# One decoder layer on one core: the Strassen units of the input projection in two passes, one for each token half

## The chip, the core and the metric

The program runs on one core of a Trainium2 chip. The metric is the device time of one execution in microseconds (us), less is better. The engines are TensorE (PE in the profile; its weight loads are listed apart as PEld), VectorE (DVE), ScalarE (ACT), GpSimd (POOL) and SyncE (SP), which issues nearly all DMAs of this kernel. Each engine works through its own instructions in order; the DMAs that SP issues are carried out by 16 DMA engines while SP goes on.

## What is computed

One hybrid layer on 2048 tokens of width 1024, in float32. The part that the change touches is the normalisation, the big input projection and the attention branch that works beside it:

```python
h = rms_norm(x, norm_w[layer])
proj = h @ w_in[layer]                    # 1024 x 9224
(dn_qkv, dn_z, dn_b, dn_a, swa_q, swa_k, swa_v, swa_z, gates) = jnp.split(proj, split_points, axis=-1)
...
sq = partial_rope(rms_norm(grp(swa_q), q_norm_w[layer][:, None, :]), cos, sin)
sk = partial_rope(rms_norm(grp(swa_k), k_norm_w[layer][:, None, :]), cos, sin)
sv = grp(swa_v)
for gi, (window, dilation) in enumerate(SWA_GROUPS):   # (128, 1), (512, 4), (2048, 16)
    o_g, lse_g = dilated_window_attention(sq[:, :, gi], sk[:, :, gi], sv[:, :, gi], window, dilation)
...
merged = jax.nn.sigmoid(g_dn) * y_dn + jax.nn.sigmoid(g_swa) * y_swa
x = x + merged @ w_out[layer]
```

## The kernel before

**Products in three matmuls.** A float32 operand is split into a high part (a copy into a rounded format, made by ACT) and a low part (the difference, made by DVE or POOL). A product is then three matmuls: high by high, high by low, low by high. All products of the projection are made so.

**Stage 1, the first unit** (`first_unit`, L412 to L500): 16 tiles of 128 tokens, in the order `ORDER`, which takes tiles of the two quarters of a token half alternately. For each tile x is loaded twice, once by rows (`xt`, a single buffer, for the sum of squares, `x_nat` L117 and `x_stat` L129) and once by channels (`xc`, `x_chan` L122). The row factor goes through a diagonal matrix (`x_diag` L136) and a matmul with ones (`x_rows` L140) to DVE, which scales `xc` (`x_scale` L146). The scaled tile is split (`x_high` L164, `x_low`), multiplied with the columns of the values of attention group 2 (24 matmuls with 256 or 264 columns a tile), and combined with its partner tile into the sums S1 to S4 (`x_sums`, `x_put`). A token half has eight such operands, A11 to A22 and S1 to S4, in high and low parts of 1 MB each. Those of the first half (p = 0) stay in SBUF in `hh` and `hl` (place by `SLOT`), A21 apart, which goes to DRAM like everything of the second half (p = 1), L172, L206 and L207; seven of the first half are written to DRAM as well (`save` L98).

**Stage 2, sixteen units** (`seq`, `unit`): a unit makes 512 columns for one token half with Strassen's scheme in Winograd's form, seven products (`PROD`) of 48 matmuls with 256 columns (L391), so 336 a unit. The token half p alternates: two units of p = 0, five of p = 1, six of p = 0, three of p = 1. In the last unit before each change of p every product, once done, loads the other half's operand into its place from DRAM (`restore` L102); after the last unit the half that is missing comes back for stage 3. The weights of the products are computed two products ahead (`w_ahead`): four loads a unit (`w_load` L253), four sums and differences on DVE (`w_sums` L259), seven high parts on ACT (`w_high` L275) and seven low parts (`w_low` L282), three on DVE and four on POOL, into a ring of four places. Each column block is thus loaded and split twice, once for each token half. Query and key units normalise their result: squares on ACT (L326), a power on POOL (L327, L329), a scaling on DVE (L334), the rotation on POOL in two halves of four instructions each (`turn`, L346 to L349), then a store (L350).

**Attention beside it.** `hook` counts a tick after every six matmuls and then runs what is due. `att_loop` gives each attention item its four pieces (load and transposes, scores, transposes of p, product with v) in steps of three phases; a step takes four ticks, delays (1, 2, 1). `att_ready` lists the items of a head once its columns are there: group 2 after p = 1, group 1 after p = 0 (which comes after p = 1 there), group 0 for each half.

**Stage 3** (`cunits`, L659 to L661): 36 units of 128 columns by 2048 tokens, each with 96 matmuls of 512 columns, for the DeltaNet branch and the gates; its weights are loaded and split by `w128` into an own pool, which opens when the pools of stage 2 are closed. Beside it run the rest of the attention, the small vectors of the DeltaNet (`ab_math`, L693 on), its chunk inverses and its scan; then the output stage (L1170 to L1189).

PE, ACT, DVE and POOL run in the order in which the program is written in stages 1 and 2 (`pinned`); the order on SP is made by a scheduler.

## Time and profile before

| what | value |
|---|---|
| time, median of 3 runs | 2518.11 us (2513.8 to 2520.08) |
| the profiled execution, its time | 2515.84 us |
| its span, first to last instruction | 2513.9 us, granted PE clock 0.965 |
| stage 1: first matmul with x at 10.5 us, last at about 191 us | 16 tiles |
| stage 2: L391 from 191.8 us to about 1081 us | 16 units |
| stage 3: first L659 at 1109.7 us | 36 units |
| DMA traffic | 413.15 MB, 164 GB/s over the span |

Busy times count an instruction from its start to its end. The matmuls of PE overlap, so a PE that is always busy can still be given work faster or slower; the number of matmuls in a stretch of known length shows the pace better. An entry such as "idle before, releaser" names what ended the wait of an engine. The wait tables list, for a waiting engine and line, who released it, the total time, how often, and the longest.

### The profile page before, as it was taken

How to read it: one execution, taken by the hardware profiler on the slowest of the kernel's cores; microseconds unless marked ns; L12 is line 12 of the kernel's file. 1: busy time of each engine (PE TensorE's matmuls, PEld its weight loads, DVE VectorE, ACT ScalarE, POOL GpSimd, SP SyncE). 2: the span in 40 equal slices, each digit the busy share in tenths (PEclk: the TensorE clock that was granted, in tenths of full speed). 3: DMA queues.
4: the chain of work that ended last, by engine and by line, in shares of the span. 5: the costliest groups of instructions: out<-in, count | busy, mean ns of one | idle time of the engine just before them, and what ended most of it. 6: DMA issues, size and time to landing. Idle time of an engine off the chain costs nothing.

```text
span 2513.9 us, 43806 instructions
## 1 busy us (share of the span) xinstructions
PE 2330.1 (93%) x15184; PEld 2106.3 (84%) x15184; DVE 1389.9 (55%) x2882; ACT 959.6 (38%) x2976; POOL 1066.5 (42%) x1754
## 2 busy tenths in 40 slices
PE   7649799989999989969899999999999999999999
PEld 7649799979999889958677888888888878898998
DVE  6435466655565555652487777699824451444431
ACT  5324344543455554633566665111233322211110
POOL 5426884552852552630085566111223321443342
PEclk8879899999999999979999999999999999999999
DMA  8993835486344674563345444322377663655442
GB/s 256 303 346 113 320 119 153 134 314 180 104 143 135 218 255 136 164 196 105 107 128 132 127 118 109 110 72 76 112 197 213 187 195 117 185 153 179 148 134 80
DMA packets 460116, 413.15 MB, mean 164 GB/s; under 512 B 63544, under 2 KB 416120, under 8 KB 451064
## 3 DMA queue, kind: packets, MB, share of 16 engines
q1 hardware_dynamic: 459608, 410.29, 53.6%
q8 instruction: 121, 1.98, 0.3%
q14 instruction: 99, 0.81, 0.1%
q10 hardware_dynamic: 288, 0.07, 0.0%
HBM read 260.01 MB, written 150.24 MB: 163 GB/s over the span
## 4 chain that ended last, share of the span: by engine, by line
PE 58%; DMA 6%; POOL 5%; DVE 3%; ACT 3%; issue 2%; SPq 0%; POOLq 0%; ACTq 0%; DVEq 0%
PE mm L391 10%; PE mm L659 8%; PE mm L661 8%; PE mm L660 8%; PE mm L1189 2%; PE mm L1187 2%; PE mm L1188 2%; PE mm L1170 2%; PE mm L1172 2%; PE mm L1171 2%; DMA gcb<-gcscr 2%; DMA qk<-qks 2%; PE tp L523 1%; PE po L565 1%; POOL kql L863 1%
## 5 line engine op out<-in xcount | busy, mean ns | idle before, releaser
L659 PE MATMUL mm<-hh,wh 128*128 128x512 f32 x1152 | 466.9, 405 | 0.0
L661 PE MATMUL mm<-hh,wl 128*128 128x512 f32 x1152 | 456.5, 396 | 0.0
L660 PE MATMUL mm<-hl,wh 128*128 128x512 f32 x1152 | 452.7, 393 | 0.0
L391 PE MATMUL mm<-wh,hh 128*128 128x256 f32 x896 | 274.2, 306 | 9.3 <-ACT wh L275 9.3
L391 PE MATMUL mm<-wl,hh 128*128 128x256 f32 x896 | 259.4, 290 | 16.1 <-POOL wl L282 15.2
L391 PE MATMUL mm<-hh 128*128 128x256 f32 x896 | 270.1, 301 | 1.9 <-ACT hh L275 1.9
L84 POOL TENSOR_TENSOR wl<-raw,wh 128x512 fp32r<-128x512 f32 x72 | 104.0, 1457 | 388.1 <-ACT wh L83 387.8
L391 PE MATMUL mm<-hl,hh 128*128 128x256 f32 x896 | 254.6, 284 | 6.4 <-POOL hl L282 6.4
L391 PE MATMUL mm<-wh,hl 128*128 128x256 f32 x896 | 259.3, 289 | 0.0
L661 PEld LDWEIGHTS mm<-hh,wl 128*128 128x128 f32 x1152 | 217.8, 189 | 47.8 <-POOL wl L84 0.4
L391 PE MATMUL mm<-hh,hl 128*128 128x256 f32 x896 | 254.5, 284 | 0.0
L659 PEld LDWEIGHTS mm<-hh,wh 128*128 128x128 f32 x1152 | 218.6, 190 | 41.5 <-ACT wh L83 0.4
L660 PEld LDWEIGHTS mm<-hl,wh 128*128 128x128 f32 x1152 | 218.3, 190 | 41.6
L391 PEld LDWEIGHTS mm<-wl,hh 128*128 128x128 f32 x896 | 176.7, 197 | 17.0 <-POOL wl L282 15.8
L391 PEld LDWEIGHTS mm<-wh,hh 128*128 128x128 f32 x896 | 177.2, 198 | 9.5 <-ACT wh L275 9.5
L391 PEld LDWEIGHTS mm<-hl,hh 128*128 128x128 f32 x896 | 172.6, 193 | 6.8 <-POOL hl L282 6.8
L391 PEld LDWEIGHTS mm<-wh,hl 128*128 128x128 f32 x896 | 175.9, 196 | 0.0
L391 PEld LDWEIGHTS mm<-hh 128*128 128x128 f32 x896 | 172.6, 193 | 2.1 <-ACT hh L275 2.1
L391 PEld LDWEIGHTS mm<-hh,hl 128*128 128x128 f32 x896 | 171.6, 192 | 0.0
L545 DVE CUSTOM_DVE_ANT_0 sc<-sc,mask 128x128 f32<-128x128 f32 (+1 forms) x192 | 71.5, 372 | 162.7 <-PE sc L543 59.3
L549 ACT ACTIVATE p<-sc,ol 128x128 f32<-128x128 f32 (+1 forms) x192 | 81.4, 424 | 205.6 <-DVE ol L545 204.6
L1170 PE MATMUL mm<-oh,hh 128*128 128x256 f32 x512 | 143.9, 281 | 1.7 <-DVE gt L1174 1.7
(299 smaller groups left out, 5969.2 us busy)
## 6 DMA issues: line engine op xcount, KB each, us to landing
qk<-qks SPq DMA_DIRECT2D x196, 128.0 KB, 2.5
wr<-in_w_in_dram SPq DMA_DIRECT2D x96, 256.0 KB, 3.5
qks<-rec SPq DMA_DIRECT2D x96, 256.0 KB, 2.2
raw<-in_w_in_dram SPq DMA_DIRECT2D x72, 256.0 KB, 3.3
gscr<-gt SPq DMA_DIRECT2D x64, 256.0 KB, 2.4
gt<-gscr SPq DMA_DIRECT2D x64, 256.0 KB, 3.4
v<-vs SPq DMA_DIRECT2D x196, 64.0 KB, 2.3
oscr<-ol SPq DMA_DIRECT2D x192, 65.0 KB, 2.2
```

The lines of the kernel that those rows point to most:

```text
L84: eng.tensor_tensor(out=l, in0=raw, in1=h.bitcast(F32), op=ALU.subtract)
L391: mm = lambda x, y, **kw: nc.tensor.matmul(o, x, y, skip_group_check=True, **kw)
L545: nc.vector.tensor_tensor_reduce(out=sc[:, 256 + lo:256 + hi], in0=sc[:, lo:hi], in1=self.mask[:, slot * P + lo:slot * P + hi], scalar=3e3 ...
L549: nc.scalar.activation(p[:, lo:hi], sc[:, 256 + lo:256 + hi], AF.Exp, bias=ol[:, 128:129], scale=-1.0, accum_out=ol[:, 129:130])
L659: nc.tensor.matmul(pr, wh[:, k, :], a, start=(k == 0), stop=False)
L660: nc.tensor.matmul(pr, wh[:, k, :], b, start=False, stop=False)
L661: nc.tensor.matmul(pr, wl[:, k, :], a, start=False, stop=(k == KT - 1))
L1170: nc.tensor.matmul(o, self.wbh[:, k, ms], oh[:, k, :], start=(k == b * 4), stop=False)
L1171: nc.tensor.matmul(o, self.wbh[:, k, ms], ol[:, k, :], start=False, stop=False)
L1172: nc.tensor.matmul(o, self.wbl[:, k, ms], oh[:, k, :], start=False, stop=(k == b * 4 + 3))
L1187: nc.tensor.matmul(pr, mh[:, k, cs], self.woh[:, k, hs], start=(k == 0), stop=False)
L1188: nc.tensor.matmul(pr, mh[:, k, cs], self.wol[:, k, hs], start=False, stop=False)
```

## The change

**All units of one token half, then of the other.** The order becomes: first unit of p = 0 (8 tiles), eight units of p = 0, first unit of p = 1 (8 tiles), eight units of p = 1. x is split into its operand places at the first unit of each half, so operands are neither saved for the second half nor restored between units; only A21 of both halves and A11, A12, A22 of p = 0 are written to DRAM, for stage 3. `x_plan` sets the ticks of the x work; for p = 1 it begins during the last unit of p = 0 and uses tiles of the weight pool for `xc`.

**Split weights parked in DRAM.** In the units of p = 0 each high and low part is written to DRAM after the split (`park`, 112 stores of 512 KB); the units of p = 1 load them into the ring instead of loading and splitting `w_in` again. The first unit of p = 1 loads and splits its four blocks anew.

**Smaller parts.** The rotation is four POOL instructions of double width instead of eight. In the units of p = 0 the low part of T1 moves from POOL to DVE. Attention steps take three ticks instead of four in the units of p = 1 (`fast`); group 1 is taken up partly after p = 0. The first weights of stage 3 are loaded and split during the last unit, into the ring. The two transposes of `ab_math` stand ahead of the two copies. `hold`, one ring of six tiles, replaces several small pools.

```diff
@@ where the order of units is set
-        self.seq = [(0, "qk", 2, (0, 1)), (0, "qk", 2, (2, 3)), (1, "qk", 2, (0, 1)), (1, "qk", 2, (2, 3)),
-                    (1, "v", 1, None), (1, "qk", 1, (0, 1)), (1, "qk", 1, (2, 3)),
...
+        order0 = [("v", 1, None), ("qk", 1, (0, 1)), ("qk", 1, (2, 3)), ("v", 0, None), ("qk", 0, (0, 1)), ("qk", 0, (2, 3)),
+                  ("qk", 2, (0, 1)), ("qk", 2, (2, 3))]
+        order1 = order0[6:] + order0[:6]
+        self.seq = [(0, *o) for o in order0] + [(1, *o) for o in order1]
...
             for u in range(len(self.seq)):
+                if u == 7:
+                    self.x_plan(self.tick + 56, 1)
+                if u == 8:
+                    self.first_unit(1)
+                    self.fast = True
                 self.unit(u)
@@ w_low: the parking
+        eng = eng or (self.nc.gpsimd if name in ("T2", "T3", "T4") else self.nc.vector)
...
+        if u != "f":
+            def park():
+                for x, a in enumerate((h, l)):
+                    self.nc.sync.dma_start(dr(self.wdr[7 * self.pair[u] + PROD_I[name]][x], 0, [[1024, P], [256, 4], [1, 256]]),
+                                           a.bitcast(F32))
+            self.at(2, park)
@@ w_ahead: the units of p = 1, and the first weights of stage 3
+        if gi >= 120:
+            if gi == 120:
+                self.c_load(0)
+            elif gi == 121:
+                self.c_split(0)
             return
+        u, i = self.where(gi)
+        if u != "f" and self.seq[u][0]:
+            h, l = self.W[gi] = tuple(a[:, :, :256] for a in self.ring[gi % 4])
+            for x, a in enumerate((h, l)):
+                self.nc.sync.dma_start(a.bitcast(F32), dr(self.wdr[7 * self.pair[u] + i][x], 0, [[1024, P], [256, 4], [1, 256]]))
+            return
@@ unit: no restore between units
-            elif nxt != p:
-                self.restore(nxt, op, *SLOT[op])
@@ x_plan (new), ticks of the x work of tile idx of half p
+            early = t - 4 if p and idx == 1 else t
+            if p or idx > 1:
+                on(early - 18, lambda m=m: self.x_stat(m))
+                on(early - 14, lambda m=m: self.x_diag(m))
...
+            if p or idx:
+                on(early - 11, lambda m=m: event(m))
...
+            if idx % 2:
+                on(t + 2, lambda m=m: self.x_sums(m))
@@ att_loop
-            self.at((1, 2, 1)[ph], lambda: self.att_loop((ph + 1) % 3))
+            self.at(1 if self.fast else (1, 2, 1)[ph], lambda: self.att_loop((ph + 1) % 3))
@@ ab_math
                 nc.tensor.transpose(pt[:64, j * P:(j + 1) * P], self.ab[:, j * 4:j * 4 + 4, :].rearrange("p h t -> p (h t)"),
                                     self.ident)
+            for j, x in enumerate((B, A)):
                 nc.vector.tensor_copy(x, pt[:64, j * P:(j + 1) * P])
```

Three places show how the instructions move. The first is SP during the change of token half. Before, in the second and third unit, SP issues the operands of the other half (`hh`, `hl` from `opd1`, 128x2048 each) between the weight loads (`wr`) and the result stores (`qks`):

```order
L102 DMA hh<-opd1A_109 128x2048
L102 DMA hl<-opd1A_110 128x2048
L102 DMA hh<-opd1S_119 128x2048
L102 DMA hl<-opd1S_120 128x2048
L102 DMA hh<-opd1A_111 128x2048
L102 DMA hl<-opd1A_112 128x2048
L253 DMA wr<-in_w_in_dram 128x4x128 x4
L350 DMA qks_86<-rec 128x2x256 x2
L102 DMA hh<-opd1S_121 128x2048
L102 DMA hl<-opd1S_122 128x2048
```

In the change no operand is loaded between units; in the units of p = 1 SP issues the parked weights (`wdr`, into the ring places `w_222` and `w_223`, or `hh` and `hl`) between the loads and stores of the attention items (`qk`, `v`, `oscr`):

```order
L311 DMA w_222<-wdr_123 128x4x256
L311 DMA w_223<-wdr_124 128x4x256
L619 DMA oscr<-ol 128x130
L565 DMA qk<-qks_86 128x256
L566 DMA v<-vs_92 128x128
L619 DMA oscr<-ol 128x130
L565 DMA qk<-qks_86 128x256
L566 DMA v<-vs_92 128x128
L311 DMA hh<-wdr_125 128x4x256
L619 DMA oscr<-ol 128x130
L311 DMA hl<-wdr_126 128x4x256
```

What moved: 14 operand loads of 1 MB at each of three places are gone, and 112 loads of 512 KB are spread over the eight units of p = 1.

The second place is SP in the first unit. Before, two `xc` loads stand together ahead of an `xt` load:

```order
L117 DMA xt<-in_x_dram 128x1024
L500 DMA vs_92<-rec 128x512
L172 DMA opd0A_97<-xh 512x1x128
L172 DMA opd0A_98<-xl 512x1x128
L122 DMA xc<-in_xcol_dram 128x1024 x2
L117 DMA xt<-in_x_dram 128x1024
L500 DMA vs_92<-rec 128x512
L98 DMA opd0A_93<-hh 128x2048
```

Now, at the same depth of the first unit, they are issued one by one between the `xt` loads:

```order
L132 DMA xc<-in_xcol_dram 128x4x256
L125 DMA xt<-in_x_dram 128x1024
L550 DMA vs_92<-rec 128x512
L132 DMA xc<-in_xcol_dram 128x4x256
L189 DMA opd0A_97<-hold 512x1x128
L189 DMA opd0A_98<-hold 512x1x128
L125 DMA xt<-in_x_dram 128x1024
L550 DMA vs_92<-rec 128x512
```

What moved: an `xt` load no longer stands behind a pair of `xc` loads, and the stores of the second half's operands (L172, L206, L207) are not in this unit any more.

The third place is PE at the end of the units. Before, the last product (L391) is followed by attention pieces, the transposes of `ab_math` (L693, L746) and only then by the first matmul of stage 3 (L659):

```order
L391 MATMUL mm<-hh,hl 128x256
L564 MATMUL po<-v,pT 128x128
L565 MATMUL po<-v,pT 128x128
L523 MATMUL tp<-ident,qk 128x128 x2
L556 MATMUL tp<-ident,p 128x128 x2
L693 MATMUL tp<-ident,ab 64x128
L541 MATMUL sc<-kq 128x256
L542 MATMUL sc<-kq 128x256
L543 MATMUL sc<-kq 128x256
L564 MATMUL po<-v,pT 128x128
L565 MATMUL po<-v,pT 128x128
L693 MATMUL tp<-ident,ab 64x128
```

Now the matmuls of stage 3 (L717 to L719) follow the last product (L422) at once, and the transposes of `ab_math` (L752) stand together behind twelve of them:

```order
L422 MATMUL mm<-hh 128x256
L422 MATMUL mm<-hl,hh 128x256
L422 MATMUL mm<-hh,hl 128x256
L605 MATMUL tp<-ident,p 128x128 x2
L717 MATMUL mm<-hh,w_222 128x512
L718 MATMUL mm<-hl,w_222 128x512
L719 MATMUL mm<-hh,w_223 128x512
```

What moved: stage 3 begins with weights that are in the ring already, and nothing of the closing pools stands ahead of it on PE. In the whole program PE has 169 attention items ahead of stage 3 now, and 156 before.

More of the change, by code (lines that the diff above doesn't have):

```diff
@@ L154, in x_home @@
             op = f"A{tok + 1}{half + 1}"
-            if p == 0 and op != "A21":
+            if op != "A21":
                 h, l = (a[:, :, j * P:(j + 1) * P] for a in self.slot(op))
             else:
-                h = self.xp.tile([P, 4, P], F32R, name="xh", bufs=4)
-                l = self.xp.tile([P, 4, P], F32R, name="xl", bufs=4)
+                h, l = (self.held().rearrange("p (a c) -> p a c", c=P) for _ in range(2))
             out.append((op, h, l))
@@ L270, in w_sums, with w_name @@
             sub(t2, r.pop((u, "B21")), t2)
+    def w_name(self, gi):
+        u, i = self.where(gi)
+        return (u, FN[i]) if u == "f" else (u, PROD[i][3])
     def w_high(self, gi):
-        u, i = divmod(gi, 7)
-        h, l = self.W[gi] = tuple(a[:, :, :256] for a in self.ring[gi % 4])
-        self.nc.scalar.activation(h, self.raw[u, PROD[i][3]][:, :, :256], AF.Copy)
+        u, name = self.w_name(gi)
+        w = 264 if u == "f" and name[2] == "1" else 256
+        h, l = self.W[gi] = tuple(a[:, :, :w] for a in self.ring[gi % 4])
+        self.nc.scalar.activation(h, self.raw[u, name][:, :, :w], AF.Copy)
@@ L360, in evict @@
         if i == 0:
-            t = hold["p1", b] = self.up.tile([P, 512], F32, name="p1", bufs=2)
+            t = hold["p1", b] = self.held().bitcast(F32)
             nc.scalar.activation(t, pr, AF.Copy)
@@ L364, in evict @@
             n = "u2" if i == 1 else "u3"
-            t = hold[n, b] = self.up.tile([P, 512], F32, name=n, bufs=2)
+            t = hold[n, b] = self.held().bitcast(F32)
             nc.vector.tensor_tensor(out=t, in0=pr, in1=hold["p1", b], op=ALU.add)
@@ L424, in first_unit @@
             self.x_home(0)
-            ent = dict(zip(names, self.ring))
-            width = lambda n: 264 if n[2] == "1" else 256
-            high = lambda n: nc.scalar.activation(ent[n][0][:, :, :width(n)], self.raw["f", n][:, :, :width(n)], AF.Copy)
-            low = lambda n, e: e.tensor_tensor(out=ent[n][1][:, :, :width(n)], in0=self.raw["f", n][:, :, :width(n)],
-                                               in1=ent[n][0][:, :, :width(n)].bitcast(F32), op=ALU.subtract)
             self.x_scale(0, rows, 0, 4)
@@ L432, in first_unit @@
             self.x_low(0, 0, nc.vector)
[L433 to L436 removed]
+            self.w_high(0)
+            self.w_low(0, nc.vector)
+            self.w_high(1)
+            self.w_low(1, nc.gpsimd)
             self.x_scale(0, rows, 4, 8)
@@ L439, in first_unit @@
             self.x_low(0, 1, nc.vector)
-            high("B21")
-            low("B21", nc.vector)
+            self.w_high(2)
+            self.w_low(2, nc.vector)
             self.x_stat(1)
@@ new lines, in f_start, with first_unit @@
+        self.x_plan(self.tick, 0)
+        self.at(30, lambda: [self.w_load(0, n) for n in ("B11", "B12", "B22", "B21")])
+    def first_unit(self, p):
+        nc = self.nc
+        g0 = 60 * p
+        if p:
+            self.w_ahead(62)
+            self.w_ahead(63)
+        ms = range(8 * p, 8 * p + 8)
+        parts = [(m, half) for m in ms for half in range(2)]
+        for x in ((0, 12) if p else (12,)):
+            parts[x + 1], parts[x + 2] = parts[x + 2], parts[x + 1]
+        prs = {}
+        ws = [self.W.pop(g0 + j) for j in range(2)]
+        for n, (m, half) in enumerate(parts):
+            t = ORDER[m]
+            if half == 0:
+                prs[m] = [self.ps.tile([P, 512], F32, name="mm", bufs=4) for _ in range(2)]
+            if half and len(ws) < 4:
+                ws += [self.W.pop(g0 + j) for j in (2, 3)]
+            for c in range(2):
+                wh, wl = ws[2 * half + c]
+                w = 256 if c else 264
+                o = prs[m][c][:, :w]
+                _, h, l = self.xs[m][half]
+                for k in range(4):
+                    nc.tensor.matmul(o, h[:, k, :], wh[:, k, :w], start=(half == 0 and k == 0), stop=False)
+                    nc.tensor.matmul(o, h[:, k, :], wl[:, k, :w], start=False, stop=False)
+                    nc.tensor.matmul(o, l[:, k, :], wh[:, k, :w], start=False, stop=(half == 1 and k == 3))
+                    if k % 2:
+                        self.hook()
+            if n == 13:
+                if p:
+                    self.w_ahead(64)
+                    self.w_ahead(65)
+                else:
+                    for c in (4, 5):
+                        self.w_sums(c)
+                        self.w_high(c)
+                        self.w_low(c, nc.vector)
+            if half:
+                pr = prs.pop(m)
+                self.xs.pop(m)
@@ L664, in cunits @@
                 fn(n, pr)
-                if pos == 0 and u + 1 < len(units):
-                    w = self.w128(units[u + 1][0])
+                if pos == 0 and u + 1 < len(fns):
+                    self.c_load(u + 1)
+                    self.c_split(u + 1)
     def flush(self):
```

329 lines of the change are left out of this document (159 added, 170 removed), and 3 rows, old and new, of the table psa.

## The prediction

> **What bounds the kernel now.** I read the page first, its busy shares and its slices of PE.
>
> ```profile
> span 2513.9 us, 43806 instructions
> PE 2330.1 (93%) x15184; PEld 2106.3 (84%) x15184; DVE 1389.9 (55%) x2882; ACT 959.6 (38%) x2976; POOL 1066.5 (42%) x1754
> PE   7649799989999989969899999999999999999999
> ```
>
> PE is the bound, and its idle time lies in the first 45% of the span, where all parts of the change lie. So I next cut the trace into the stages: first unit, sixteen units, the seam to stage 3, and the start of stage 3. The columns are the stretch, its length, then busy time and count of PE, PEld, DVE, ACT, POOL, the granted PE clock, the DMA share and GB/s.
>
> ```profile
> 13.00:191.80 178.80, 111.15 (x795) 108.57 (x793) 81.51 (x171) 71.94 (x157) 78.81 (x79) 0.81 0.92 302
> 191.80:1081.50 889.70, 831.02 (x6761) 816.51 (x6761) 507.72 (x1262) 424.34 (x1462) 504.65 (x988) 0.97 0.56 178
> 1081.50:1109.70 28.20, 7.17 (x27) 4.57 (x25) 9.14 (x29) 6.04 (x26) 11.04 (x36) 0.58 0.85 242
> 1109.70:1250.00 140.30, 137.57 (x758) 111.83 (x757) 60.60 (x194) 58.84 (x170) 10.40 (x8) 0.99 0.38 109
> ```
>
> Busy time hides lost time here, since the matmuls overlap; counts show it. Single stretches of 25 us:
>
> ```profile
> 150.00:175.00 25.00, 8.86 (x55) 8.86 (x56) 8.62 (x21) 5.93 (x14) 5.07 (x4) 0.66 0.98 337
> 275.00:300.00 25.00, 21.41 (x165) 21.04 (x165) 16.07 (x31) 12.10 (x45) 18.74 (x39) 0.93 1.03 366
> 550.00:575.00 25.00, 20.19 (x162) 18.86 (x160) 16.14 (x44) 11.99 (x48) 20.62 (x50) 1.00 0.90 302
> 675.00:700.00 25.00, 19.86 (x152) 19.66 (x151) 9.37 (x26) 10.42 (x38) 19.72 (x40) 0.86 0.55 168
> 725.00:750.00 25.00, 24.52 (x205) 23.87 (x204) 11.80 (x34) 11.11 (x30) 12.59 (x19) 1.00 0.66 186
> 975.00:1000.00 25.00, 25.00 (x214) 24.85 (x213) 13.70 (x39) 13.39 (x45) 13.12 (x21) 1.00 0.52 140
> 1050.00:1075.00 25.00, 25.00 (x215) 24.84 (x214) 16.39 (x48) 15.16 (x56) 13.57 (x33) 1.00 0.78 250
> ```
>
> A full PE does 214 matmuls in 25 us, 0.1168 us each. That is my unit price. The first unit's 768 matmuls are worth 89.7 us and take from 10.5 to 191 us; at 150 us PE does 55 where it could do 214, beside a DMA share of 0.98. In the units 6761 matmuls are worth 790 us of 889.7, so 100 us are lost: at the changes of token half (275, 550) and where POOL is nearly full without one (675). The seam does 27 matmuls in 28.2 us. PE's own waits name the same places:
>
> ```profile
> PE tp L140 <- ACT dg L136: 58.4, 11, 17.1
> PE tp L556 <- ACT p L549: 19.2, 22, 4.4
> PE mm L391 <- POOL wl L282: 15.2, 3, 5.2
> PE tp L693 <- DVE s L721: 15.2, 1, 15.2
> PE mm L391 <- ACT wh L275: 9.3, 1, 9.3
> PE mm L391 <- POOL hl L282: 6.4, 2, 4.7
> ```
>
> **The change part by part.** All terms are against the profiled execution (2515.84 us, span 2513.9); it lies 2.3 us below the median of 2518.11, so a prediction for it holds for the median within that.
>
> *First unit of p = 0.* Its pace is that of the row norm: `xt` has one buffer, so load, square and next load form a chain. SP's issues of `xt` and ACT's squares (L129) in the steady part of before:
>
> ```profile
> 44.66 0.38 SPq L117 DMA_DIRECT2D xt<-in_x_dram  x1
> 50.41 1.06 ACT L129 ACTIVATE xt<-xt 128x1024 f32<-128x1024 f32 x1 [3.14 <-DMA xt<-in_x_dram]
> 51.59 0.33 SPq L117 DMA_DIRECT2D xt<-in_x_dram  x1
> 56.50 1.04 ACT L129 ACTIVATE xt<-xt 128x1024 f32<-128x1024 f32 x1
> 59.46 0.81 SPq L122 DMA_DIRECT2D xc<-in_xcol_dram  x2
> 60.37 0.38 SPq L117 DMA_DIRECT2D xt<-in_x_dram  x1
> 67.14 1.06 ACT L129 ACTIVATE xt<-xt 128x1024 f32<-128x1024 f32 x1 [4.16 <-DMA xt<-in_x_dram]
> ```
>
> Issue to issue is 6.93 us (44.66 to 51.59) when nothing stands ahead; the third `xt` waits behind a pair of `xc` and takes 8.8. Two tiles take 16.7 us. The change keeps the one buffer but issues `xc` singly, so I take 7.0 us a tile. The square of the eighth tile was at 56.5 and stays near it; in the new tick plan it stands 26 ticks of six matmuls, 18.2 us, ahead of the unit's end: **end at 74 us**. Worth of 384 matmuls: 44.9, so 18.6 us remain lost after the start at 10.5.
>
> *First unit of p = 1.* Same chain, but begun 27 ticks ahead, beside the last unit of p = 0. From the second tile's square to the last there are 52 ticks (36 us of matmuls) for six turns of 7.0 us: 6 us late, and about 2 for the two parked weight loads that are asked for only with two parts left. **8 us lost** on 44.9. Together the two first units lose 27 us where one lost 91.
>
> *Sixteen units.* 5376 matmuls stay, 627.9 us. Attention had 6761 - 5376 = 1385 matmuls for 156 items; 13 more items stand ahead of stage 3, with 11 matmuls each (two, two, three and four, as the trace counts them), and 36 further transposes of loads made ahead: 1564, 182.7 us. What is lost beside that falls for two reasons. The 42 operand loads of 1 MB go, and with them the stretches like 275 and 550. And POOL is relieved:
>
> ```profile
> L84 POOL TENSOR_TENSOR wl<-raw,wh 128x512 fp32r<-128x512 f32 x72 | 104.0, 1457 | 388.1 <-ACT wh L83 387.8
> L329 POOL TENSOR_TENSOR st<-st,mhalf 128x4 f32<-128x4 f32 x96 | 99.4, 1036 | 8.0
> L346 POOL TENSOR_TENSOR t<-rec,rope 128x64 f32<-128x64 f32 x192 | 78.9, 411 | 10.8 <-DVE rec L334 1.4
> L282 POOL TENSOR_TENSOR wl<-wr,wh 128x1024 fp32r<-128x1024 f32 x32 | 76.3, 2384 | 107.8 <-ACT wh L275 57.2 <-DMA qk<-qks 23.3 <-DMA v<-vs 20.8
> L347 POOL TENSOR_TENSOR t<-rec,rope 128x64 f32<-128x64 f32 x192 | 68.8, 358 | 0.0
> L349 POOL TENSOR_TENSOR rec<-t,t 128x32 f32<-128x32 f32 x192 | 55.4, 289 | 0.0
> ```
>
> A query-key unit asks POOL for eight rotations of 2 x (411 + 358 + 2 x 289) = 2.69 us, eight powers of about 1.3 and four low parts of 2.38: 41.5 us, more than the unit's 336 matmuls, 39.2. The double-width instruction is not in the trace; it costs between the old one (a rotation 1.35) and two old ones (2.69). By the slope from L84 to L282, 0.93 us for 512 elements, 64 more elements are 0.12 and 32 more 0.06, so I take 1.70, near the lower end. That gives 31 us a unit in p = 0 (three low parts) and 24 in p = 1 (none): POOL has slack. DVE gains the low part of T1 in p = 0 and loses all sums and low parts in p = 1; at 508 of 890 us it hides that. `hold` can make DVE wait for PE once a tile pair, two ticks, at worst 11 us over eight pairs; I take nothing, as DVE has half its time free.
>
> What stays lost: dense attention without a change of half or a full POOL runs at 205 to 215 in 25 us (725, 975, 1050), 2% below full. I take 3% of 389 us in p = 0, 12 us, and, for the shorter attention steps, 5% of 422 in p = 1, 21 us. From scores to the transposes of p there are now two ticks (1.4 us of matmuls) instead of three, so the wait on `ACT p` (19.2 us in 22 waits) must grow; the bounds are nothing and half a tick for each of p = 1's 105 items, 37 us.
>
> *Parking.* Stores and loads themselves stand beside the matmuls; the cover is the 39.2 us of a unit. Sizes:
>
> ```profile
> qk<-qks SPq DMA_DIRECT2D x196, 128.0 KB, 2.5
> v<-vs SPq DMA_DIRECT2D x196, 64.0 KB, 2.3
> oscr<-ol SPq DMA_DIRECT2D x192, 65.0 KB, 2.2
> wr<-in_w_in_dram SPq DMA_DIRECT2D x20, 512.0 KB, 6.1
> hl<-opd1S SPq DMA_DIRECT2D x8, 1024.0 KB, 9.1
> ```
>
> A unit of p = 0 stores 14 x 512 KB, loads four blocks and stores 2.1 MB of results; three of them also save 2.1 MB of operands: 13.6 MB. At the 337 GB/s of the saturated stretch that is 40.4 us for 39.2 of matmuls. So the first three units of p = 0 sit at the DMA limit, the others at 11.5 MB and about 9 attention items lower. Bounds: nothing, since the stores may trail by 20 us before their ring place is written again, and 57 us (below). I take **10 us**.
>
> [...]
>
> Loads in p = 1 (7.3 MB a unit, 230 GB/s with attention) lie below the 250 GB/s at which PE was full (1050). A ring place is free three products, 16.8 us, ahead of its use, against 6.1 us to land: nothing.
>
> *Sum up to the seam.* 10.5 + 89.8 + 627.9 + 182.7 + 18.6 + 8 + 12 + 21 + 10 = 980.5, for 1081.5: **-101**.
>
> *Seam.* Stage 3's first weights are ready and its matmuls stand at once behind the last product. The first group's three PSUM tiles and 96 matmuls cover the closing pools; the second weights are issued behind the same late stores as before and may be some us late. Of 25 idle us I take **-20** (bounds 0 and -25). The 13 items done earlier leave stage 3, which is full at its start (137.57 of 140.3): 13 x 11 x 0.1168 = **-17**. Later stages are the same instructions.
>
> 2515.8 - 101 - 20 - 17 = 2378, given as **2380 us**.
>
> **The rivals.** *DMA is the bound in p = 0.* About 115 MB are moved there; at 250 GB/s, the most beside a full PE, 460 us instead of 403: 2437. For it: 13.6 MB a unit. Against: 337 and 366 were reached. *The short attention steps cost their upper bound*: 2380 + 37 = 2417; against it, ACT and DVE lose the splitting there. *Slower: the parked weights come late in p = 1.* SP issues them in one line with result stores that wait on POOL:
>
> ```profile
> SPq L350 <- POOL rec L349: 191.6, 68, 7.0
> ```
>
> If SP is late by two of the longest such waits, 14 us, a load lands 20.1 us after its place is free, 3.3 us late, in each of 56 products: 185 us, 2565. It decides from 13.2 us of lateness (2.5 us a product) on; the usual wait is 191.6/68 = 2.8. *Nothing comes of it*: the x chains stay at the 8.4 us a tile of the trace (+22), the units keep their 100 lost us because DMA takes the place of the operand loads (+57), the seam stays (+20) and attention costs its bound (+37): 2380 + 136 = 2516.
>
> **How the numbers follow.** Chances: forecast 0.68, DMA bound 0.15, attention 0.08, late weights 0.05, nothing 0.04. A measurement tells about 0.3% (7.5 us) from no change. Faster: 0.68 + 0.15 + 0.08 = 0.91; same 0.04; slower 0.05. The low end takes the first units' 27 us and the seam mostly won, 2330; the high end holds the DMA rival and part of both, 2450.
>
> **What would show it.** First unit of p = 0 ending near 74 us and that of p = 1 lasting near 53; no stretch below 190 matmuls in 25 us in the units; POOL rotations near 1.7 us; the wait on `ACT p` below 40 us; first 512-column matmul near 982 us. Wrong would be: DMA share at 1.0 through the units of p = 0 with PE waiting for `wr`, PE waiting for `wdr` loads in p = 1, or a first unit of p = 1 beyond 70 us.

## The result and the profile after

The changed kernel takes 2400.9 us (median of 4 runs, 2396.77 to 2405.99) where the kernel before took 2516.57 in the same session: a ratio of 0.9541, 95% interval 0.9517 to 0.9564, so 4.6% faster. The forecast was 2380, 21 us lower. The profiled execution is the slowest of the four, 2405.99 us; a second timing of the same kernel, beside the last experiments, gave 2398.43 us (ratio 0.9538, 0.9522 to 0.9554) with a profiled span of 2394.1. Where two numbers stand for the changed kernel below, they are of these two profiles or timings. Every time below is the median of its executions, without one of the run with all three edits of the first unit, which took 3743 us at a granted clock of 0.556.

From the page of after, the span, the engines and the slices of PE:

```profile
span 2404.2 us, 43315 instructions
PE 2317.2 (96%) x15218; PEld 2092.4 (87%) x15218; DVE 1345.1 (56%) x2854; ACT 914.8 (38%) x2941; POOL 886.5 (37%) x1330
PE   8999999989999999899999999999999999999999
```

Most of the holes of before are filled. Three of the 40 slices, each 60 us long, stay below 9: the first one, the ninth (481 to 541 us, with most of the first unit of p = 1) and the seventeenth (962 to 1022, the end of the units). The same trace cut into stages (stretch, length, busy time and count of PE, PEld, DVE, ACT and POOL, granted clock, DMA share, GB/s): first unit, units of p = 0, first unit of p = 1, units of p = 1 with the seam, start of stage 3.

```profile
10.50:74.60 64.10, 51.91 (x399) 50.45 (x399) 44.36 (x91) 36.32 (x78) 39.66 (x37) 0.92 0.97 325
74.60:497.60 423.00, 408.16 (x3336) 401.49 (x3337) 257.46 (x592) 214.95 (x715) 195.08 (x295) 0.98 0.83 264
497.60:557.80 60.20, 53.43 (x398) 52.50 (x397) 45.48 (x93) 34.12 (x87) 52.59 (x59) 0.91 0.71 218
557.80:1018.10 460.30, 436.66 (x3635) 428.70 (x3633) 219.67 (x707) 187.63 (x779) 127.56 (x277) 0.99 0.79 244
1018.10:1150.00 131.90, 121.95 (x625) 96.45 (x626) 58.65 (x169) 47.28 (x137) 17.61 (x26) 0.97 0.49 137
```

Set against the forecast, in us (the last column is the run with larger rings, explained below; the forecast's units of p = 1 are 422 + 21, its seam 28.2 - 20, its remainder the 1404.2 of before less 17):

| stretch | forecast | after | second profile | larger rings |
|---|---|---|---|---|
| start and first unit of p = 0 | 74 | 74.6 | 74.7 | 74.6 |
| units of p = 0 | 411 | 423.0 | 420.7 | 406.5 |
| first unit of p = 1 | 53 | 60.2 | 58.8 | 59.1 |
| units of p = 1 and seam | 451 | 460.3 | 456.3 | 448.7 |
| the rest | 1387 | 1386.1 | 1383.6 | 1381.4 |

The 18 to 28 us by which the two profiles exceed the forecast lie in two places: the units, and the first unit of p = 1. In p = 1 the loss of the units is some 6 us larger than the table shows, since the seam came out at 2.2 us where 8.2 were forecast. PE's own waits, which the prediction went by, hardly show the loss:

```profile
PE tp L605 <- ACT p L598: 17.5, 17, 2.6
PE tp L153 <- ACT dg L149: 13.6, 7, 3.6
PE tp L572 <- DMA qk<-qks: 10.7, 7, 4.5
PE mm L422 <- ACT ab L548: 4.5, 1, 4.5
```

The row norm's wait fell from 58.4 to 13.6 us, and PE's waits for split weights in the units from 30.9 to 0.8; the wait on `ACT p` is no larger than before. But `ACT p` has a chain behind it. DVE's score instruction writes the `ol` tile, `ol` has three buffers, and a buffer is free only when its store to `oscr` has landed. DVE's wait for that store, in the units of p = 0 and then of p = 1:

```profile
DVE sc L594 <- DMA oscr<-ol: 10.0, 4, 4.2
DVE sc L594 <- DMA oscr<-ol: 22.4, 13, 3.1
```

One of the four in p = 0, in order of time (start, length, engine, line, instruction, and in brackets how long the engine had waited for what):

```profile
361.82 0.43 DVE L594 CUSTOM_DVE_ANT_0 sc<-sc,mask 128x256 f32<-128x256 f32 x1 [4.25 <-DMA oscr<-ol]
362.34 0.47 ACT L598 ACTIVATE p<-sc,ol 128x256 f32<-128x256 f32 x1 [2.36 <-DVE ol L594]
362.96 0.44 PE L605 MATMUL tp<-ident,p 128*128 128x128 f32 x2 [2.07 <-ACT p L598]
363.15 0.48 PE L422 MATMUL mm<-w,hh 128*128 128x256 f32 x2
...
365.02 0.53 PE L591 MATMUL sc<-kq 128*128 128x256 f32 x1 [0.80 <-DVE kq L580]
...
365.57 0.63 PE L422 MATMUL mm<-w,hh 128*128 128x256 f32 x2
365.99 0.41 PE L422 MATMUL mm<-w,hl 128*128 128x256 f32 x1
366.21 0.63 PE L422 MATMUL mm<-w,hh 128*128 128x256 f32 x2
```

The late store becomes 2.07 us of waiting on PE, and 0.80 more for DVE, which is late too. Then comes a second price that no wait shows: three matmuls now start every 0.64 us (365.57 to 366.21), 0.21 each, where a full PE does one in 0.117, and this lasts until 368 us. The trace has the granted clock at 0.50 from 365.1 to 368.5 us, and at 1.00 ahead of that. In the 25 us around it PE did 159 matmuls instead of some 210, at a mean granted clock of 0.93.

### The profile page after: what moved, and what is told of

It reads as the page before. It is cut to its first block, busy times and chain, and to the rows that moved or that the text cites. A ratio compares the mean times of both kernels' runs of the same rounds, so it can differ in the third digit from the quotient of the medians.

```text
span 2404.2 us, 43315 instructions
## 1 busy us (share of the span) xinstructions
PE 2317.2 (96%) x15218; PEld 2092.4 (87%) x15218; DVE 1345.1 (56%) x2854; ACT 914.8 (38%) x2941; POOL 886.5 (37%) x1330
## 4 chain that ended last, share of the span: by engine, by line
PE 68%; DMA 10%; DVE 6%; issue 5%; POOL 5%; ACT 4%; SPq 1%; POOLq 0%; DVEq 0%; ACTq 0%
PE mm L422 17%; PE mm L717 9%; PE mm L718 9%; PE mm L719 9%; DMA qk<-qks 2%; PE mm L1247 2%; PE mm L1249 2%; PE mm L1248 2%; PE mm L1230 2%; PE mm L1232 2%; PE mm L1231 2%; DMA oscr<-ol 2%; PE tp L572 1%; DMA oc<-oscr 1%; PE po L614 1%
## 5 line engine op out<-in xcount | busy, mean ns | idle before, releaser
L717 PE MATMUL mm<-hh,w 128*128 128x512 f32 x1152 | 464.1, 403 | 5.2 <-DVE gt L1142 3.0
L719 PE MATMUL mm<-hh,w 128*128 128x512 f32 x1152 | 458.2, 398 | 0.0
L718 PE MATMUL mm<-hl,w 128*128 128x512 f32 x1152 | 457.9, 398 | 0.0
L422 PE MATMUL mm<-w,hh 128*128 128x256 f32 x1792 | 353.6, 294 | 5.0 <-ACT ab L548 4.5
L422 PEld LDWEIGHTS mm<-w,hh 128*128 128x128 f32 x1792 | 278.9, 192 | 5.4 <-ACT ab L548 4.7
L422 PE MATMUL mm<-hh 128*128 128x256 f32 x896 | 271.4, 303 | 0.0
L717 PEld LDWEIGHTS mm<-hh,w 128*128 128x128 f32 x1152 | 220.7, 192 | 51.3 <-DVE gt L1142 3.4
L719 PEld LDWEIGHTS mm<-hh,w 128*128 128x128 f32 x1152 | 217.3, 189 | 46.9
L422 PE MATMUL mm<-w,hl 128*128 128x256 f32 x896 | 254.6, 284 | 0.0
L718 PEld LDWEIGHTS mm<-hl,w 128*128 128x128 f32 x1152 | 217.9, 189 | 41.9
L422 PE MATMUL mm<-hl,hh 128*128 128x256 f32 x896 | 253.7, 283 | 0.3 <-POOL hl L290 0.3
L422 PE MATMUL mm<-hh,hl 128*128 128x256 f32 x896 | 253.7, 283 | 0.0
L88 POOL TENSOR_TENSOR w<-raw,w 128x512 fp32r<-128x512 f32 x70 | 102.5, 1466 | 385.0 <-ACT w L87 382.1
L422 PEld LDWEIGHTS mm<-hl,hh 128*128 128x128 f32 x896 | 171.9, 192 | 0.5 <-POOL hl L290 0.5
L422 PEld LDWEIGHTS mm<-hh 128*128 128x128 f32 x896 | 171.9, 192 | 0.0
L422 PEld LDWEIGHTS mm<-w,hl 128*128 128x128 f32 x896 | 171.1, 191 | 0.0
L422 PEld LDWEIGHTS mm<-hh,hl 128*128 128x128 f32 x896 | 171.1, 191 | 0.0
L594 DVE CUSTOM_DVE_ANT_0 sc<-sc,mask 128x128 f32<-128x128 f32 (+1 forms) x192 | 71.6, 373 | 163.2 <-PE sc L592 58.8
L1232 PE MATMUL mm<-oh,hl 128*128 128x256 f32 x512 | 142.9, 279 | 0.0
```

The lines of the kernel that those rows point to most:

```text
L88: eng.tensor_tensor(out=l, in0=raw, in1=h.bitcast(F32), op=ALU.subtract)
L422: mm = lambda x, y, **kw: nc.tensor.matmul(o, x, y, skip_group_check=True, **kw)
L594: nc.vector.tensor_tensor_reduce(out=sc[:, 256 + lo:256 + hi], in0=sc[:, lo:hi], in1=self.mask[:, slot * P + lo:slot * P + hi], scalar=3e3 ...
L717: nc.tensor.matmul(pr, wh[:, k, :], a, start=(k == 0), stop=False)
L718: nc.tensor.matmul(pr, wh[:, k, :], b, start=False, stop=False)
L719: nc.tensor.matmul(pr, wl[:, k, :], a, start=False, stop=(k == KT - 1))
```

## The experiments

**Theory.** The units lose time because the small stores of attention land later under the new DMA traffic than the three-deep `ol` ring allows. **Rivals**: the DMA queues themselves are full; the three-tick step costs the time in p = 1; POOL or SP's line hold things up.

**Larger rings.**

```
-        qk = a["qk"] = self.sp.tile([P, 2, P], F32, name="qk", bufs=3)
+        qk = a["qk"] = self.sp.tile([P, 2, P], F32, name="qk", bufs=4)
-        ol = a["ol"] = sp.tile([P, 130], F32, name="ol", bufs=3)
+        ol = a["ol"] = sp.tile([P, 130], F32, name="ol", bufs=6)
```

> The changed kernel with six `ol` tiles instead of three and four `qk` tiles instead of three; nothing else. In the changed kernel's profiled execution (2404.2 us span) the units of p = 0 last 423 us, the first unit of p = 1 60 us, the units of p = 1 458 us, and DVE's score waits 32.4 us for the `oscr` store of an `ol` tile three items back. Theory A (the units lose time because attention's small stores and loads land later and PE then waits for `p` and runs at a lower clock): DVE's wait for `oscr` goes to under 3 us, PE's wait on `ACT p` from 17.5 us to under 11, and the two groups of units become 10 to 20 us shorter together: 2380 to 2392 us. Rival B (the loss comes from the full DMA queues and the SP order themselves, and attention's wait is only where it shows): the wait on `oscr` goes and another takes its place, units within 5 us of 881, time 2396 to 2406.

Measured: 2372.35 us, ratio 0.9440 (0.9422 to 0.9457), 26 to 29 us below the changed kernel. The gain goes the way of theory A and is larger than theory A expected, in the time and in the units (22 to 28 us). Units of p = 0, first unit, units of p = 1 with the seam:

```profile
74.60:481.10 406.50, 400.49 (x3337) 395.85 (x3338) 257.90 (x593) 216.42 (x717) 197.65 (x295) 1.00 0.86 275
481.10:540.20 59.10, 51.79 (x399) 50.94 (x398) 44.26 (x91) 32.93 (x85) 50.72 (x59) 0.94 0.70 216
540.20:988.90 448.70, 433.69 (x3634) 428.69 (x3632) 222.57 (x707) 187.64 (x779) 127.52 (x276) 0.99 0.80 250
```

Over its whole span, DVE's wait for `oscr` and PE's for `p`:

```profile
DVE sc L594 <- DMA oscr<-ol: 2.5, 2, 1.4
PE tp L605 <- ACT p L598: 5.4, 6, 2.2
```

With as many matmuls (3337) the units of p = 0 become 16.5 us shorter: PE's idle time falls from 14.8 (423.00 - 408.16) to 6.0, and its busy time from 408.2 to 400.5, the granted clock rising from 0.98 to 1.00. So about half of the loss was waiting and half slower matmuls. The two worst stretches of the units of p = 0 in after stand against the same ones here; first after, then the larger rings:

```profile
175.00:200.00 25.00, 20.89 (x168) 20.18 (x167) 13.32 (x39) 11.91 (x42) 10.62 (x20) 0.96 1.03 340
350.00:375.00 25.00, 20.73 (x159) 19.94 (x158) 13.90 (x37) 13.27 (x51) 7.48 (x14) 0.93 0.78 249
```

```profile
175.00:200.00 25.00, 23.87 (x203) 23.71 (x202) 16.52 (x45) 14.47 (x54) 12.03 (x22) 1.00 1.07 355
350.00:375.00 25.00, 24.75 (x208) 24.15 (x207) 20.52 (x53) 17.96 (x69) 17.29 (x31) 1.00 0.88 277
```

At 175 us the DMA engines are full in both kernels, and with the larger rings PE does 203 matmuls beside 355 GB/s. That takes the ground from the rival of a DMA bound: full DMA engines did not hold PE up, the small transfers of attention that came late did. In p = 1 the larger rings do not clear everything: four stretches of its units stay between 177 and 189 matmuls, and PE's waits for the loads of `qk`, 5.9 us there, are the largest that are left.

**The stores of parking alone.**

```
-        if u != "f":
+        if u == 0:
             def park():
...
-dr(self.wdr[7 * self.pair[u] + i][x], 0, [[1024, P], [256, 4], [1, 256]]))
+dr(self.wdr[i][x], 0, [[1024, P], [256, 4], [1, 256]]))
```

> The changed kernel with the split weights parked for the first unit only; p = 1 loads the first unit's blocks in every unit, as many bytes as before. Left out: 49 of the 56 parked pairs, so seven of the eight units of p = 1 compute with another unit's weights. About 51 MB of stores go out of p = 0. Theory A (DMA traffic of p = 0 is what lengthens its units): they last 409 to 414 us instead of 423, DVE's wait for `oscr` there under 3 us instead of 10, the units of p = 1 stay within 5 us of 458, time 2386 to 2393. Rival B (the loss of p = 0 beyond full PE is attention's own chain and the start of POOL's work, whatever DMA moves): the units of p = 0 stay within 4 us of 423, time 2396 to 2404.

Measured: 2382.22 us, ratio 0.9475 (0.9456 to 0.9495), theory A and some 3 us below its bands; units of p = 0:

```profile
73.90:480.40 406.50, 400.56 (x3337) 395.36 (x3338) 255.19 (x593) 216.66 (x717) 195.00 (x295) 1.00 0.49 149
```

That is the same 406.5 us as with the larger rings, at half the DMA share. Taking the traffic away and giving the rings room are two ways to one result, and doing both (below) brings no more: 407.3 us. So in p = 0 what the stores of parking cost, they cost through the rings of attention. The link is the time from issue to landing of the `oscr` store (minimum, median, maximum): in after for p = 0 and p = 1, then in this run for p = 0.

```profile
DMA to landing us min/median/max: 1.8/3.1/7.5
DMA to landing us min/median/max: 1.6/3.9/8.5
```

```profile
DMA to landing us min/median/max: 1.6/2.1/4.1
```

In the kernel before it was 2.4 in the units. In p = 1, where this run loads as much as the changed kernel, the units stayed at 457.2 us, within what was expected.

How little room the ring has can be worked out. In p = 1 a tick is 458.3/448 = 1.02 us, and three steps of three ticks, 9.2 us, pass before a buffer is due again. It is held for four ticks from score to PV (the product with v; 4.1 us), the copy (0.29), the wait for SP (some 0.7 on the average, pairing DVE's copies with SP's issues) and 3.9 to land: 9.0 us. In p = 0 the same count is 5.7 + 0.29 + some 0.9 + 3.1 = 10.0 of 11.3. This is an estimate from medians and averages. They just fit, with 0.2 and 1.3 us to spare, so a store that lands well behind its median (the latest took 8.5 and 7.5 us) is a stall: 13 of the 105 in p = 1 and 4 of the 64 in p = 0.

**The short attention step.**

```
-            self.at(1 if self.fast else (1, 2, 1)[ph], lambda: self.att_loop((ph + 1) % 3))
+            self.at((1, 2, 1)[ph], lambda: self.att_loop((ph + 1) % 3))
```

> The changed kernel with attention's step at four ticks in p = 1 too, as it is in p = 0. Some 26 items of 11 matmuls at 0.1168 us, 33 us, then move behind the units into stage 3. Theory A (the three-tick step costs p = 1 time, as predicted with 5% of 442 us): the units of p = 1 become 33 us shorter by the moved items and 10 to 20 us more by the step, stage 3 takes 33 us more, time 2382 to 2392. Rival B (the step costs nothing by itself): the units become 33 us shorter and no more, stage 3 33 us longer, time 2396 to 2406. Rival C: stage 3 has not room for 49 items beside its first matmuls, PE shows gaps there, and the time is above 2410.

Measured: 2406.51 us, ratio 0.9578 (0.9558 to 0.9598). Units of p = 1 with the seam, and the start of stage 3:

```profile
557.00:961.90 404.90, 395.49 (x3351) 392.95 (x3349) 192.89 (x602) 156.95 (x674) 128.83 (x277) 1.00 0.82 257
961.90:1150.00 188.10, 168.58 (x903) 130.48 (x904) 86.15 (x273) 79.88 (x242) 16.06 (x22) 0.95 0.48 139
```

None of the three theories fits as a whole. The units are 51 to 55 us shorter for 284 matmuls less (33 us), so the short step does cost 18 to 22 us there, as A had it; all behind the seam takes 1441.3 us instead of 1383.6 to 1386.1, 55 to 58 more for the same 33, so stage 3 gives 22 to 25 us back, as C had it (PE idle for 19.5 of 188.1 us). The time is at the upper edge of B's. So the short step costs in p = 1 what it saves in stage 3: the whole time is 6 to 8 us longer without it, and the two ratios overlap. All this is with the three-tile ring. The larger rings take 8 to 12 us of p = 1 back at three ticks, and no run has four ticks with them, so how much of the 18 to 22 us is the ring's is not known.

**Without parking, and without parking but with larger rings.** In p = 1 the plain weights are loaded, summed and split as in p = 0.

```
-        if u != "f":
+        if False:
             def park():
...
-        if u != "f" and self.seq[u][0]:
+        if False:
...
-                    self.w_ahead(64)
-                    self.w_ahead(65)
+                    self.at(1, lambda: self.w_high(64))
+                    self.at(3, lambda: self.w_low(64))
+                    self.at(4, lambda: (self.w_load(8, "B21"), self.w_sums(65)))
+                    self.at(5, lambda: self.w_high(65))
+                    self.at(7, lambda: self.w_low(65))
```

> The changed kernel without parking: no split weights are stored in p = 0, and the units of p = 1 load the plain weights, build their sums and split them again as in p = 0. DMA moves 51 MB of stores and some 42 MB of loads less; ACT, DVE and POOL get the split of 56 blocks back (a high part, a low part, three sums a unit). The kernel without the stores but with the parked loads had 406.5 us in the units of p = 0 (423.0 with the stores) and 457 in the units of p = 1. Theory A (parking costs more, through attention's late stores, than the splitting it saves): units of p = 0 404 to 410 us, units of p = 1 with the seam 445 to 457, time 2370 to 2386. Rival B (the splitting makes POOL and DVE late in p = 1 by as much as parking cost in p = 0): units of p = 1 with the seam 470 us or more, time 2395 to 2415.

> The changed kernel without parking (p = 1 loads plain weights and splits them again) and with six `ol` and four `qk` tiles. Without parking and with the small rings the units lasted 406.7 us in p = 0 and 470.3 in p = 1 with the seam; with parking and the larger rings 406.5 and 448.7. Theory A (parking costs nothing once the stores of attention have room, and saves p = 1 the splitting): p = 0 404 to 409, p = 1 462 to 470, time 2385 to 2397. Rival B (the larger rings take the waits away without parking too, and parking is worth nothing): p = 1 446 to 455, time 2370 to 2378.

Measured: 2396.08 us (ratio 0.9528, 0.9514 to 0.9542) and 2390.9 us (0.9507, 0.9493 to 0.9521). Units of p = 0, then of p = 1 with the seam, without parking:

```profile
74.50:481.20 406.70, 400.95 (x3337) 395.76 (x3338) 255.17 (x593) 216.43 (x717) 194.42 (x295) 0.99 0.44 129
541.10:1011.40 470.30, 440.92 (x3635) 429.57 (x3633) 295.57 (x770) 237.56 (x837) 195.74 (x302) 0.99 0.51 151
```

and with the larger rings too:

```profile
74.00:481.30 407.30, 401.57 (x3337) 396.46 (x3338) 255.08 (x593) 216.49 (x717) 194.45 (x294) 0.99 0.44 129
540.50:1002.60 462.10, 436.05 (x3634) 426.58 (x3632) 295.06 (x770) 237.74 (x837) 195.91 (x301) 1.00 0.51 154
```

Parking as it is in the change is worth nothing that these runs can tell: the units of p = 0 are 14 to 16 us shorter without it (406.7), those of p = 1 10 to 14 longer, and the two ratios overlap. The first run falls to its rival B. With the larger rings in both, parking is worth 18.5 us (2390.9 - 2372.35; 462.1 against 448.7 in p = 1): theory A of the second run.

The four runs also show where parking acts through the rings. In p = 0 the larger rings bring 14 to 16 us with parking and nothing without it (407.3 against 406.7). In p = 1 they bring 8 to 12 us with parking and 8 without it (462.1 against 470.3), although the `oscr` store there lands in 2.3 us at the median without parked loads and in 3.9 with them. So it is not shown that the parked loads make the price of the ring in p = 1; the difference, at most 4 us, is no larger than that between the two profiles of the changed kernel. The kernel without parking has the splitting in p = 1 instead, so the comparison is not a clean one.

**The rotation in eight instructions.** The function `turn` as before the change.

```
+            for a in range(2):
+                rope = self.rope[:, t + a, 0, :]
...
-            t1 = self.up.tile([P, 4, 2, 16], F32, name="t1", bufs=1)
+                t1 = self.up.tile([P, 2, 2, 16], F32, name="t1", bufs=1)
```

> The changed kernel with the rotation in eight POOL instructions again instead of four. A rotation takes 1.78 us in the changed kernel and took 2.69 before; eight of them make 7.3 us more POOL work in a query-key unit of some 50 us: about 39 us instead of 32 in p = 0 and 31 instead of 24 in p = 1. Theory A (POOL's relief is a large part of the units' gain): units 10 to 25 us longer together, waits on POOL's `st` and low parts back, time 2411 to 2426. Rival B (with the operand loads gone and attention in every unit POOL is off the path at 39 us too): units within 5 us of 883, time 2396 to 2406; only the first unit of p = 1, where POOL is full, gets 2 to 5 us longer.

Measured: 2427.73 us, ratio 0.9659 (0.9643 to 0.9675): 27 to 29 us more than the changed kernel: theory A, 2 us above its band for the time. Units of p = 0, first unit, units of p = 1 with the seam:

```profile
73.80:509.80 436.00, 411.10 (x3336) 403.52 (x3337) 256.17 (x593) 216.30 (x717) 227.93 (x467) 0.97 0.81 257
509.80:573.20 63.40, 53.17 (x399) 52.22 (x397) 42.51 (x91) 33.05 (x85) 54.78 (x79) 0.92 0.66 205
573.20:1043.50 470.30, 442.18 (x3635) 433.79 (x3633) 217.03 (x707) 188.10 (x779) 156.13 (x451) 0.98 0.77 239
```

POOL is busy for 52% of p = 0 and a third of p = 1, and yet a leaner POOL is a quarter of the change's gain. Part of the way is seen: in p = 0 PE waits 10.9 us, in two waits, for low parts that POOL makes, where it waited 0.8 us in after, and DVE's wait for `oscr` went from 10.0 to 15.2 us there and from 22.4 to 37.0 in p = 1. How much of the 27 to 29 us goes through that ring was not separated.

**Stage 3's first weights late.**

```
-            if gi == 120:
-                self.c_load(0)
-            elif gi == 121:
-                self.c_split(0)
...
+        self.c_load(0)
+        self.c_part(0, 0)
+        self.c_part(0, 1)
```

> The changed kernel with stage 3's first weights loaded and split only when stage 3 begins, as before the change. Theory A (the seam is won by the early load alone): the gap between the last product and the first 512-column matmul grows from 1.7 us to 20 to 28, time 2419 to 2427. Rival B (the closing of the pools would hide most of it, or the seam is won by the operands that stay in place): gap below 12 us, time 2401 to 2412.

Measured: 2416.86 us, ratio 0.9618 (0.96 to 0.9636), 16 to 18 us more. The seam is back:

```profile
1018.00:1042.70 24.70, 4.07 (x16) 2.93 (x17) 7.36 (x23) 4.17 (x16) 6.37 (x17) 0.56 0.85 237
```

So the early load and split make the seam by themselves: 24.7 us of gap, theory A, though the time is 2 us under its band. All behind the seam was 4 to 6 us shorter in this run.

**The first unit of p = 1: `xt` on ACT's queue, lighter POOL, both.**

```
-            self.nc.sync.dma_start(self.xt[m], dr(self.i["x"], P * ORDER[m] * D, [[D, P], [1, D]]))
+            (self.nc.scalar if m > 9 else self.nc.sync).dma_start(self.xt[m], dr(self.i["x"], P * ORDER[m] * D, [[D, P], [1, D]]))
```

```
-        nc.gpsimd.tensor_tensor(out=l, in0=s, in1=h.bitcast(F32), op=ALU.subtract)
+        eng = nc.vector if m > 7 and op in ("S3", "S4") else nc.gpsimd
+        eng.tensor_tensor(out=l, in0=s, in1=h.bitcast(F32), op=ALU.subtract)
```

> The changed kernel with the `xt` loads of the third to eighth tile of p = 1's first unit issued on ACT's DMA queue instead of SP's. In the changed kernel that unit lasts 60 us, and one `xt` load is issued 10 us after its buffer is free, behind SP rows that wait for DVE and POOL. Theory A (the head of SP's line delays the row norm): the unit lasts 50 to 55 us, ACT's wait for `xt` there under 1 us, time 5 to 10 us less, 2391 to 2396. Rival B (POOL is nearly full there, 23.8 of 25 us between 500 and 525, and the small statistics and low parts wait for POOL in any case): the unit stays at 58 us or more and the time within 3 us of 2401.

> The changed kernel with six `ol` tiles (and still three `qk` tiles), and with the low parts of S3 and S4 of p = 1's first unit on DVE instead of POOL: eight instructions of 1.4 us there. For the first edit: theory A (the `ol` tiles alone made the gain of the run with both rings) gives 404 to 409 us for the units of p = 0 and 446 to 452 for those of p = 1 with the seam; rival B (the fourth `qk` tile had a part in it) gives 412 or more and 455 or more. For the second: POOL has 52 of 60 us of work in that unit, PE waits there only for the row norm's `dg`. Theory A (POOL's line is what makes the row norm late) gives a first unit of 51 to 55 us instead of 60; rival B (the one `xt` buffer and its SP row set the pace, and POOL's load is only beside it) gives 58 to 60. Time with A and A 2366 to 2372, with A and B 2373 to 2379.

> The changed kernel with all three edits: six `ol` and four `qk` tiles, the low parts of S3 and S4 of p = 1's first unit on DVE, and the later `xt` loads of that unit on ACT's queue. Theory A (POOL and the place of `xt` in SP's line each hold the row norm up, so both have to go): first unit of p = 1 46 to 53 us, time 2360 to 2368. Rival B (the row norm has another floor, its chain of load, square, power, scale and transposes from one buffer): first unit 55 us or more, time 2367 to 2374.

> The changed kernel as it is, on the chip of the three runs below, so that they are compared with it directly. Both theories: ratio to before 0.952 to 0.957, as in its first timing (0.9541).

Measured, in the same order: 2399.76 us (ratio 0.9548, 0.9532 to 0.9565), 2381.12 (0.9467, 0.9453 to 0.9481), 2377.57 (0.9454, 0.9438 to 0.947), and 2398.43 for the changed kernel beside the last two. The unit lasted 58.7, 60.8 and 60.7 us against 60.2 and 58.8: closest to rival B each time, no edit made it clearly shorter. The second and third run are also 2 to 4 us slower than the bands that went with rival B, and 5 to 9 slower than the run with the larger rings. POOL fell to 43.2 of 60.7 us with both:

```profile
482.70:543.40 60.70, 52.99 (x398) 51.92 (x397) 48.65 (x98) 33.15 (x85) 43.20 (x53) 0.92 0.69 212
```

and `xt` on ACT's queue only changed the line that it stands in. In the run with all edits ACT squares a tile, and issues the next `xt` 4 us after the square has ended, behind an eviction that waits for PE:

```profile
508.03 1.04 ACT L142 ACTIVATE xt<-xt 128x1024 f32<-128x1024 f32 x1
...
512.88 0.38 ACT L550 ACTIVATE rec<-mm 128x256 f32<-128x256 f32 x1 [2.10 <-PE mm L532]
513.06 0.34 ACTq L125 DMA_DIRECT2D xt<-in_x_dram  x1
```

So POOL's load is not the cause, and SP's line alone is not; that the load of `xt` waits in some engine's line is not excluded, since the edit only moved it to another one. Which hop of the chain (load, square, power, scale, transposes, high part) sets the pace stays open. For the rings these runs settle one thing: with six `ol` tiles alone the units lasted 410.6 and 448.8 us (just over theory A's band in p = 0, inside it in p = 1), so most of the gain in p = 0 and all of it in p = 1 is that ring's. In p = 0 the fourth `qk` tile brings some 4 us more (406.5 and, in the run with all edits, 406.3).

**The rings in the kernel before.** The same two `bufs` in the kernel before the change.

> The kernel before the change with six `ol` tiles instead of three and four `qk` tiles instead of three, the edit that took 28 us from the changed kernel (ratio to before 0.9440 instead of 0.9541). In the trace of before DVE waits 42.1 us in 17 waits for `oscr`, and PE 19.2 us on `ACT p`. Theory A (the three-tile ring was too short already, and the loss was hidden in the 100 us that the units of before lose): 15 to 30 us faster, ratio 0.988 to 0.994. Rival B (it is the change that made the stores late: 3.4 us to land instead of 2.2 at the median, by the parking traffic and the shorter step): within 6 us, ratio 0.9975 to 1.0025; then the changed kernel's shortfall against the prediction comes from the change itself.

Measured: 2502.79 us, ratio 0.9952 (0.9936 to 0.9968), 12 us faster: between A and B. DVE's wait for `oscr` in the units went from 36.8 us (42.1 in the whole span) to

```profile
DVE sc L545 <- DMA oscr<-ol: 2.5, 2, 1.4
```

so the short rings cost 12 us before the change already and cost 26 to 29 after it. Some 14 to 17 us of that are the change's own doing. A longer wait in the units (36.8 against 32.4 us) was worth less there: PE's wait on `ACT p` fell from 17.2 to 4.6 us, and its wait for the loads of `qk` rose from 13.9 to 25.0.

The kernel with the larger rings is the fastest of all here: 2372.35 us against 2400.9 and 2398.43 for the changed kernel and 2514.34 for the kernel before beside it.

## Why the prediction was nearly right, and where it was not

**What bounds, and the first unit of p = 0.** Right. The unit ended at 74.6 us for 74, so the turn of 7 us a tile and the plan of ticks were well read.

**The amount of work.** Right: 169 items ahead of stage 3 (DVE's copies of `po`: 64 in p = 0 and 105 in p = 1), 6971 matmuls in the units where 5376 + 1564 = 6940 were forecast.

**Parking: "Stores and loads themselves stand beside the matmuls".** This is the step that failed. Stores and loads were costed by their bytes alone, 10 us for p = 0 and "nothing" for p = 1. The matmuls did stand beside full DMA engines; what grew was the time to land of attention's small stores, 2.4 us before, 3.1 and 3.9 after, against a ring of three tiles whose size the prediction never looked at, although the trace of before had the wait (42.1 us of DVE, behind the quoted wait on `ACT p`). No term of the sum stood for that ring. The larger rings measure it: 14 to 16 us in p = 0, 8 to 12 in p = 1. In p = 0 it is what parking costs; that the 10 us set down for a limit of bytes came near it was luck. In p = 1 the rings cost about as much, 8 us, without the parked loads, so "nothing" for the loads is not refuted there. With the larger rings the two groups of units take 406.5 and 448.7 us where 411 and 451 were forecast, so the other terms hold as a sum; one by one not all of them were measured.

**The short step, 21 us.** The size came out, 18 to 22, but with the three-tile ring, and the ring's share in it was not separated. The sign that was named for it did not come: "the wait on `ACT p` must grow", and it went from 19.2 to 17.5. So this size may be in part luck.

**POOL.** Right in kind: the rotation took 526 + 487 + 349 + 384 ns, 1.75 us, for 1.70 estimated. No sum was set beside it; undoing it alone costs 27 to 29 us.

**First unit of p = 1: "8 us lost".** Too low by 6 to 7. From the second tile's square to the last it took 54.7 us where six turns of 7.0 were forecast: turns of 13.7, 8.2, 14.5, 6.9, 5.5 and 5.8 us. Two long turns make the loss. Why they are long stays open, see above.

**Seam and rest.** The gap went from 28.2 us to about 2, better than -20; the early load and split are worth 16 to 18 us of time. The rest fell by 18 to 21 us where 17 were forecast.

**The rivals.** The DMA bound is out: 203 matmuls stood beside 355 GB/s, where it took 250 for the most beside a full PE. Late parked weights are out: PE waited for no `wdr` load. The attention rival had its price in p = 1 alone; the loss is as large in p = 0, where the step is the old one. The test "no stretch below 190 matmuls in 25 us" was the one that spoke: 168, 188 and 159 in the units of p = 0, which all rise to 199 or more with the larger rings, and 160 to 188 in five stretches of the units of p = 1, where four below 190 remain with them.

## What to carry to other kernels

Bulk traffic added beside a latency chain is to be priced in two ways: by its bytes, and by what a longer landing time (here 2.4 us before, 3.1 and 3.9 after) does to every ring of buffers that is freed by a small transfer. Compare the time for which a buffer is held with the time until it is due again, before and after. Where the margin was 0.2 and 1.3 us, as here, more buffers brought 26 to 29 us; leaving the parking out, with the splitting back in its place, brought 2 to 5, which is not clear of the noise. And follow a wait on the bounding engine back through the engines ahead of it, since its first cause may stand under another engine's name.

## What the runs showed of the hardware

A transfer of 65 KB, the store to `oscr`, took 2.1 us to land at the median with the DMA engines at a share of 0.49 (units of p = 0, parking for the first unit only), and in the changed kernel 3.1 at 0.83 (units of p = 0) and 3.9 with parked loads at 0.79 (units of p = 1). The stretch with the lowest share had the smallest median, 1.8 us below the largest.

In the trace of after, behind a wait of PE of 2.07 us and one of 0.80, the granted clock was 0.50 from 365.1 to 368.5 us, and matmuls started 0.21 us apart instead of 0.117. In the 3.41 us ahead of that, from 361.69 to 365.11, PE was busy for 1.35 us.

The whole trace of after shows what counted. Its granted clock is 1.00 or 0.50, in 28 spells by turns. All but the last, which the end of the profile cuts at 3.37 us, last a multiple of 3.41 us; of the 14 at 0.50 eight last 3.41 us, four 6.83 and one 10.24. Cut the trace into stretches of 3.41 us at these changes: every one of the 13 at full clock in which PE was idle for 1.95 us or more in all was followed by half clock. Of the others, idle for 1.75 us or less, one was followed by it (1.11 us idle, at 2051 us). So in this trace waits that came to 1.95 us or more within one such stretch had 3.37 us or more at half clock behind them. What makes the clock fall is not shown by these counts.
